# Last block of a Strassen-Winograd w_down product: another order of its seven products, a table of the side engines' work by step, and a fixed order for the finish of the output rows

## The chip, the core and the metric

One NeuronCore of a Trainium2 chip runs the whole kernel as one program. The metric is the device time of one execution in microseconds (us); smaller is better. Before the change three executions took 1968.8, 1969.25 and 1969.59 us; the median, 1969.25 us, is the time before.

## What is computed

The reference is one decoder layer in fp32 on 512 real tokens and 16 meta tokens of width 2048: RMSNorm, a combined input projection, sliding-window attention beside an mLSTM, an output projection with a residual, then

```python
u = rmsnorm(h, norm_mlp)
h = h + square(relu(u @ w_up)) @ w_down        # w_down: 8192 x 2048
h = rmsnorm(h, norm_final)
return h[:, BLOCK:]                             # 512 x 2048
```

The change touches the end of `@ w_down`, the last residual add and the final RMSNorm.

## The kernel before

Every fp32 product is made from three passes on TensorE: each operand is split into a rounded part `hi` (a cast on ScalarE, line 124) and a rest `lo` (a subtraction on VectorE, line 125), and `hi*hi + hi*lo + lo*hi` is accumulated in PSUM (lines 1086, 1089, 1090).

The `w_down` product runs over 16 blocks (`BLOCKS`, numbered 0 to 15 here): 8 chunks of the 8192 rows of `w_down` times two halves of the output columns. A block is a 2x2 Strassen-Winograd product: seven products (`ORDER`) instead of eight, each in two steps, so 14 steps m = 0 to 13. One step (`product`, L1067) is 12 matmuls with 512 columns. Its results gather in four PSUM tiles called X, W, Q and, in block 15, V (allocated under the name X), and from there in four quarters c00, c01, c10, c11 of the output, each 256 token rows by 512 columns.

What goes on beside the matmuls of step m is issued by `step` (L1098), and for block 15 by `last_step` (L1161):

- The operand of step m+2 is split (`weight_operand`, L1058): `hi(m+2)` on ScalarE, then `lo(m+2)` on VectorE. In this text hi(k) and lo(k) are the halves of the operand of step k of block 15. Three buffers hold such pairs, so hi(k) waits until TensorE is done with step k-3.
- Four of the seven weight operands are sums (`weight_sum`, L1052, the tiles t1 to t4, two halves each) of weight tiles y11, y12, y21, y22, made on VectorE (L1055). The weights come by DMAs that SP (SyncE) issues: `load_rows0` (L1027, tiles `raw`) and `load_rows1` (L1034, tiles `rh`); y12 of block 15 is loaded at step 7 of block 14.
- Finished quarters are copied or added out of PSUM (`add`, L1092) and accumulated into the DRAM tensors `hd` by a DMA with accumulation that POOL issues (`accumulate`, L1095); block 14 does so for c11 at step 11, c01 at step 12 and c10 at step 0 of block 15.
- In block 15 SP reads the sums back for the final norm: `load_h1(row, j)` (L1141) loads two tiles of 128 tokens by 512 columns into h1, `load_quarter` (L1146) the two column quarters that block 15 itself still adds to. h1(0, 1) can be read only when block 14's c01 has been accumulated, h1(1, 1) after its c11. ScalarE takes the sums of squares (`squares`, L1152, at line 708) and VectorE multiplies by the norm's weights (`weigh`, L1156).

TensorE, ScalarE and VectorE run in the order in which the code issues their instructions (`manual_schedule`, L1226), but only up to step 11 of block 15. SP and POOL are ordered by the scheduler, which lets a ready instruction pass one that is not ready: in `last_step(0)` the code issues `load_quarter(0, 1)` ahead of `load_quarter(1, 1)` and `load_h1(1, 1)`, and SP takes the latter two first.

After step 11 the rest is outside that order: `finish(b)` (L1198) for the four row blocks b, each a row scale on POOL (`v`, from the partial sums of squares, L1201 and L1202), two scaled tiles on ScalarE (L1204) and two on VectorE (L1208), each with its own output DMA of 256 KB (from ScalarE's queue L1205, from SP L1209). The last product (step 12 and 13) is done for the token half t = 0 into W and for t = 1 into V, and each half is added to c10 (L1093).

```python
LAST_ORDER = (0, 1, 5, 4, 2, 6, 3)
LAST_SUM_AT = {0: ("t2", 1), 3: ("t3", 0), 5: ("t3", 1), 6: ("t4", 0), 9: ("t4", 1)}
LAST_SRC = ("y11", "y21", "t2", "t1", "y22", "t3", "t4")
```

Of the kernel before, what the change touches and what calls it, by code (L numbers as in the profile page):

```python
# [10 lines left out]
F32 = mybir.dt.float32  # L11
# [6 lines left out]
P = 128  # L18
# [66 lines left out]
def hybrid_layer(ctx, tc, io, out):  # L85
# [959 lines left out]

    LASTB = len(BLOCKS) - 1
    LAST = STEPS * LASTB
    LAST_ORDER = (0, 1, 5, 4, 2, 6, 3)
    LAST_SUM_AT = {0: ("t2", 1), 3: ("t3", 0), 5: ("t3", 1), 6: ("t4", 0), 9: ("t4", 1)}
    LAST_SRC = ("y11", "y21", "t2", "t1", "y22", "t3", "t4")  # L1050

    def weight_sum(B, t, h):  # L1052
        dst = b3s.tile([P, 1024], F32, name="s", tag="s", bufs=5)
        in0, in1 = (wts[B, n, h] for n in SUM[t])
        dve.tensor_tensor(out=dst[:], in0=in0, in1=in1, op=ALU.subtract)  # L1055
        wts[B, t, h] = dst[:]
# [10 lines left out]
    def product(g, ts=(0, 1), hs=None):  # L1067
        B, m = divmod(g, STEPS)
        c, i = BLOCKS[B][0], m // 2
        if m == 0:  # L1070
            bks[B] = [dps.tile([P, 2, 512], F32, name=n, tag=n, bufs=2 if n == "X" else 1) for n in "XWQ"]
        if B == LASTB:
            if m == 8:
                bks[B].append(dps.tile([P, 2, 512], F32, name="X", tag="X", bufs=2))
            p, n, start = LAST_ORDER[i], (0, 1, 0, 2, 3, 0, 1)[i], i in (0, 1, 3, 4, 6)
        else:
            p, n, start = ORDER[i], (0, 1, 0, 2, 0, 2, 0)[i], i in (0, 1, 3)
        out = bks[B][n]
        for t in ts:
            for h in hs or (m % 2,):  # L1080
                wh, wl = ops[g - g % 2 + h]
                hi, lo = unit[c, p, h]
                for q in range(2):
                    a, a2 = (x[:, q * HTOK + t * P : q * HTOK + (t + 1) * P] for x in (hi, lo))
                    cols = slice(q * 512, (q + 1) * 512)
                    pe.matmul(  # L1086
                        out[:, t], a, wh[:, cols], start=start and h == q == 0, stop=False, skip_group_check=True
                    )
                    pe.matmul(out[:, t], a, wl[:, cols], start=False, stop=False, skip_group_check=True)  # L1089
                    pe.matmul(out[:, t], a2, wh[:, cols], start=False, stop=h == q == 1, skip_group_check=True)  # L1090
# [7 lines left out]
    def step(g):  # L1098
# [15 lines left out]
        if m in SUM_AT:  # L1114
            weight_sum(B, *SUM_AT[m])
        elif m == 13 and B < LASTB - 1:
            weight_sum(B + 1, "t1", 0)
        if g != 1:
            weight_operand(g + 2)
        if B == LASTB - 1 and m >= 12:  # L1120
            for t, h in ((("t1", 0),), (("t1", 1), ("t2", 0)))[m - 12]:
                weight_sum(B + 1, t, h)
        for mm, row, col in ((4, 0, 0), (11, 1, 1), (12, 0, 1)):
            if m == mm:
                add(cs[B, f"c{row}{col}"][:], (W if m == 4 else Q if m == 12 else cs[B, "c10"])[:])
# [5 lines left out]
            load_rows1(B + 1)  # L1131


    h1, nfs, last_sq = {}, [], {}

    def load_nf():
        for j in range(NJ):
# [3 lines left out]
    def load_h1(row, j):  # L1141
        h1[2 * row, j], h1[2 * row + 1, j] = unit_pair(len(keys_) + 2 * j + row, F32)
        for b in (2 * row, 2 * row + 1):
            sync.dma_start(out=h1[b, j], in_=hd[j][row][:, b % 2])

    def load_quarter(row, col):  # L1146
        d = quarter(LASTB, f"c{row}{col}")
        sync.dma_start(out=d[:], in_=hd[2 + col][row][:])
        for t in range(2):
            h1[2 * row + t, 2 + col] = d[:, t]  # L1150
# [5 lines left out]
    def weigh(row, j):  # L1156
        for b in (2 * row, 2 * row + 1):
            dve.tensor_tensor(out=h1[b, j], in0=h1[b, j], in1=nfs[j][:], op=ALU.mult)

    def last_step(m):  # L1160
        X, W, Q = bks[LASTB][:3]  # L1161
        if m == 0:
            act.copy(quarter(LASTB - 1, "c10")[:], bks[LASTB - 1][0][:])
            accumulate(LASTB - 1, 1, 0)
            load_h1(0, 0)
            load_quarter(0, 1)
            load_quarter(1, 1)
            load_h1(1, 1)
            load_h1(0, 1)
            load_h1(1, 0)  # L1170
            load_quarter(1, 0)
        elif m == 2:
            act.copy(quarter(LASTB, "c00")[:], X[:])
        if m in LAST_SUM_AT and m < 6:
            weight_sum(LASTB, *LAST_SUM_AT[m])
        if m < 12:
            weight_operand(LAST + m + 2)
        if m in LAST_SUM_AT and m >= 6:
            weight_sum(LASTB, *LAST_SUM_AT[m])
        for mm, row, j in ((1, 0, 0), (3, 1, 1), (4, 0, 1), (7, 1, 0), (10, 0, 2)):  # L1180
            if m == mm:
                squares(row, j)
        for mm, row, j in ((2, 0, 0), (5, 1, 1), (6, 0, 1), (8, 1, 0)):
            if m == mm:
                weigh(row, j)
        if m == 4:
            d = cs[LASTB, "c00"]
            add(d[:], W[:])
            pool.dma_start(out=hd[2][0][:], in_=d[:], accum_op=ALU.add)
            load_quarter(0, 0)  # L1190
        elif m in (7, 8, 10):
            add(cs[LASTB, "c01"][:], (X if m == 7 else Q if m == 8 else bks[LASTB][3])[:])
        elif m == 11:
            add(cs[LASTB, "c11"][:], Q[:])
            for b in range(2):
                last_square(b, 3)

    def finish(b):  # L1198
        tok = slice(b * P, (b + 1) * P)
        v = b3.tile([P, 1], F32, name=f"v{b}")  # L1200
        pool.tensor_tensor(out=v[:], in0=last_sq[b][:], in1=part[b][:], op=ALU.add)  # L1201
        pool.tensor_tensor(out=v[:], in0=v[:], in1=mhalf[:, :1], op=ALU.pow)  # L1202
        for j in (0, 1):
            act.activation(h1[b, j], h1[b, j], AF.Copy, scale=v[:])  # L1204
            act.dma_start(out=out[tok, j * 512 : (j + 1) * 512], in_=h1[b, j])  # L1205
        for j in (2, 3):
            h = h1[b, j]
            dve.scalar_tensor_tensor(out=h, in0=h, scalar=v[:], in1=nfs[j][:], op0=ALU.mult, op1=ALU.mult)  # L1208
            sync.dma_start(out=out[tok, j * 512 : (j + 1) * 512], in_=h)  # L1209

    part = {}

    def partial(b):
        part[b] = b3.tile([P, 1], F32, name=f"part{b}")
# [2 lines left out]
    def last_square(b, j):  # L1217
        last_sq[b] = b3.tile([P, 1], F32, name=f"sq{b}")
        act.activation(junk, h1[b, j], AF.Square, accum_out=last_sq[b][:])

    load_units(4 + FB)
    load_rows0(0, 0)
# [3 lines left out]
    with tc.manual_schedule(engines={mybir.EngineType.PE, mybir.EngineType.Activation, mybir.EngineType.DVE}):  # L1226
# [15 lines left out]
        for m in range(STEPS - 2):  # L1242
            product(LAST + m)
            last_step(m)
    X, W, _, V = bks[LASTB]
    for b in range(2):
        partial(b)
        finish(b)
    add(cs[LASTB, "c11"][:], X[:])
    add(cs[LASTB, "c10"][:], X[:])  # L1250
    squares(1, 3)
    for b in range(2, NB):
        partial(b)
    for t in range(2):
        bks[LASTB][1] = (W, V)[t]
        with tc.manual_schedule(engines=MAN):
            product(LAST + 12, (t,), (0, 1))
        add(cs[LASTB, "c10"][:, t], (W, V)[t][:, t])
        last_square(2 + t, 2)
        finish(2 + t)  # L1260


def layouts(inputs):
# [70 lines left out]
```

## Time and profile before

| what | value |
|---|---|
| median of three executions | 1969.25 us |
| the profiled execution's own time | 1968.98 us |
| its span, first to last instruction | 1967.2 us |
| TensorE busy | 1948.9 us, 99% of the span |
| VectorE busy / ScalarE busy / POOL busy | 1406.0 / 1010.8 / 238.8 us |
| mean granted TensorE clock | 0.998 of full speed |

All moments below are microseconds from the start of the span, so the last block of `w_down` lies near 1915 to 1953 and the end at 1967.2. A timeline row gives the start, the duration, the engine, the line, the operation with output and inputs, the shape, how many were merged, and in brackets the idle time before it and what ended that. Instructions of one engine overlap a little, so the distance between two starts is the price of one in a row of them.

### The profile page before, as it was taken

Reading aid. Unit: us, or ns where it says so; the run is one execution under the profiler, and the core shown is the slowest. Engines: PE = TensorE matmul, PEld = TensorE weight load, DVE = VectorE, ACT = ScalarE, POOL = GpSimd, SP = SyncE. Lnnn points to the kernel's source line nnn. Section 1 sums busy time; section 2 is a strip of 40 time slices with the busy share of each in tenths; the row PEclk is TensorE's granted clock in tenths of the full one; section 3 lists DMA queues with packets and bytes.
Section 4 is the critical chain, followed back from the end, with each engine's and each line's share of the span. In section 5 each row is a group of like instructions: output and inputs, shape, how many; then the busy total and the mean of one; then the engine's idle time right before and its main releaser. Section 6 shows DMA issues by size and latency. Waiting matters only on the chain.

```text
span 1967.2 us, 30626 instructions
## 1 busy us (share of the span) xinstructions
PE 1948.9 (99%) x12240; PEld 1745.6 (89%) x12240; DVE 1406.0 (71%) x1844; ACT 1010.8 (51%) x1491; POOL 238.8 (12%) x346
## 2 busy tenths in 40 slices
PE   9999999999999999999999999999999999999997
PEld 7878989988888899999999999998888888888885
DVE  6547773233644378787878787878888988888887
ACT  4433542245533255555555555556566566555655
POOL 0112220012111023222220000001100100010010
PEclk9999999999999999999999999999999999999999
DMA  8412112211243336555554444457878888888765
GB/s 316 135 65 88 65 65 76 91 70 65 86 171 130 127 137 210 191 187 187 188 184 166 157 166 153 169 167 253 212 217 224 227 222 215 226 208 203 223 171 187
DMA packets 112752, 324.61 MB, mean 165 GB/s; under 512 B 14016, under 2 KB 50496, under 8 KB 93648
## 3 DMA queue, kind: packets, MB, share of 16 engines
q1 hardware_dynamic: 65728, 245.55, 36.5%
q0 software_dynamic: 12320, 41.95, 10.9%
q10 hardware_dynamic: 34560, 35.14, 5.5%
q8 instruction: 96, 1.57, 0.3%
q14 instruction: 48, 0.39, 0.1%
HBM read 244.45 MB, written 78.15 MB: 164 GB/s over the span
## 4 chain that ended last, share of the span: by engine, by line
PE 69%; issue 24%; POOL 3%; DVE 2%; ACT 1%; DMA 1%; POOLq 0%; DVEq 0%; SPq 0%; ACTq 0%
PE g L171 10%; PE a L778 5%; PE g L778 5%; PE a L780 5%; PE a L779 5%; PE g L780 5%; PE g L779 5%; PE g L715 3%; PE g L717 3%; PE g L716 3%; PE g L186 2%; PE g L234 2%; POOL hd L1096 2%; PE g L184 2%; PE g L185 2%
## 5 line engine op out<-in xcount | busy, mean ns | idle before, releaser
L124 ACT CAST whi<-raw 128x1024 fp32r<-128x1024 f32 x224 | 235.3, 1050 | 405.3 <-PE g L717 85.5
L125 DVE TENSOR_TENSOR wlo<-raw,whi 128x1024 fp32r<-128x1024 f32 x224 | 274.6, 1226 | 201.5 <-ACT whi L124 196.5
L125 DVE TENSOR_TENSOR wlo<-s,whi 128x1024 fp32r<-128x1024 f32 x256 | 312.9, 1223 | 110.1 <-ACT whi L124 108.7
L124 ACT CAST whi<-s 128x1024 fp32r<-128x1024 f32 x256 | 269.0, 1051 | 209.5 <-PE g L779 62.1
L171 PE MATMUL g<-s,whi 128*128 128x264 f32 x1216 | 204.9, 287 | 0.2 <-DVE qa L270 0.2
L171 PEld LDWEIGHTS g<-s,whi 128*128 128x128 f32 x1216 | 170.9, 189 | 5.4 <-issue 4.9
L1089 PE MATMUL X<-wlo,s 128*128 128x512 f32 x356 | 138.6, 389 | 0.1
L1090 PE MATMUL X<-whi,s 128*128 128x512 f32 x356 | 138.5, 389 | 0.0
L1086 PE MATMUL X<-whi,s 128*128 128x512 f32 x356 | 138.5, 389 | 0.0
L171 PE MATMUL g<-s,wlo 128*128 128x264 f32 x608 | 128.0, 287 | 0.0
L778 PE MATMUL g<-y,whi 128*128 128x256 f32 x448 | 126.0, 281 | 1.0 <-ACT whi L124 1.0
L778 PE MATMUL a<-y,whi 128*128 128x256 f32 x448 | 125.6, 280 | 0.0
L779 PE MATMUL a<-s,whi 128*128 128x256 f32 x448 | 125.4, 280 | 0.0
L780 PE MATMUL a<-y,wlo 128*128 128x256 f32 x448 | 125.3, 280 | 0.0
L780 PE MATMUL g<-y,wlo 128*128 128x256 f32 x448 | 125.3, 280 | 0.0
L779 PE MATMUL g<-s,whi 128*128 128x256 f32 x448 | 125.3, 280 | 0.0
L779 PE MATMUL a<-y,whi 128*128 128x256 f32 x448 | 125.2, 280 | 0.0
L779 PE MATMUL g<-y,whi 128*128 128x256 f32 x448 | 125.2, 280 | 0.0
L780 PE MATMUL a<-s,wlo 128*128 128x256 f32 x448 | 125.2, 279 | 0.0
L778 PE MATMUL a<-s,whi 128*128 128x256 f32 x448 | 125.1, 279 | 0.0
L780 PE MATMUL g<-s,wlo 128*128 128x256 f32 x448 | 125.1, 279 | 0.0
L778 PE MATMUL g<-s,whi 128*128 128x256 f32 x448 | 124.8, 279 | 0.0
(371 smaller groups left out, 5099.2 us busy)
## 6 DMA issues: line engine op xcount, KB each, us to landing
raw<-in_w_dram SPq DMA_DIRECT2D x144, 1024.0 KB, 5.1
rh<-in_w_dram SPq DMA_DIRECT2D x64, 512.0 KB, 5.5
hd<-c POOLq DMA_DIRECT2D x61, 512.0 KB, 5.4
fu<-fd SPq DMA_DIRECT2D x108, 256.0 KB, 4.0
fd<-d ACTq DMA_DIRECT2D x32, 512.0 KB, 3.2
fd<-fs ACTq DMA_DIRECT2D x31, 512.0 KB, 3.5
xtok<-in_x_dram SPq DMA_DIRECT2D x4, 1024.0 KB, 11.6
hs<-in_x_dram SPq DMA_DIRECT2D x16, 256.0 KB, 5.8
```

The costliest lines, as they stand in the source:

```text
L124: act.copy(dst_hi, src)
L125: dve.tensor_tensor(out=dst_lo, in0=src, in1=dst_hi.bitcast(F32), op=ALU.subtract)
L171: pe.matmul(ps[s], w, x[:, PARTS[s]], start=first and kt == 0, stop=last and kt == KT - 1,)
L715: pe.matmul(ps[b][:], a, wh, start=kt == first, stop=False)
L716: pe.matmul(ps[b][:], a, wl, start=False, stop=False)
L717: pe.matmul(ps[b][:], c, wh, start=False, stop=kt == last)
L778: pe.matmul(out, wh, ah_, start=start and q == 0, stop=False, skip_group_check=True)
L779: pe.matmul(out, wh, al_, start=False, stop=False, skip_group_check=True)
L780: pe.matmul(out, wl, ah_, start=False, stop=q == KQ - 1, skip_group_check=True)
L1086: pe.matmul(out[:, t], a, wh[:, cols], start=start and h == q == 0, stop=False, skip_group_check=True)
L1089: pe.matmul(out[:, t], a, wl[:, cols], start=False, stop=False, skip_group_check=True)
L1090: pe.matmul(out[:, t], a2, wh[:, cols], start=False, stop=h == q == 1, skip_group_check=True)
```

## The change

Block 15 gets another order of products (p4 ahead of p5; p4 and p2 add up in Q, so that V holds only the last product's second half). VectorE's work by step is written in a table, with the squares of ScalarE beside it: those of (0, 0), (0, 1), (1, 1), (1, 0), (0, 2) stood at steps 1, 4, 3, 7, 10 and now follow the cast of steps 1, 2, 4, 6, 9. Block 14 makes the first three weight sums of block 15 at steps 8, 11 and 13 instead of 12, 13 and 13. The loads at the start of block 15 are issued in another order. The finish of all rows is moved into the fixed order of the three engines: that of rows 0 and 1 begins in step 11 (`first_rows`, ahead of hi(13) and lo(13)), the rest is written out in `last_rows`.

```diff
-    LAST_ORDER = (0, 1, 5, 4, 2, 6, 3)
-    LAST_SUM_AT = {0: ("t2", 1), 3: ("t3", 0), 5: ("t3", 1), 6: ("t4", 0), 9: ("t4", 1)}
-    LAST_SRC = ("y11", "y21", "t2", "t1", "y22", "t3", "t4")
+    LAST_ORDER = (0, 1, 4, 5, 2, 6, 3)
+    LAST_SRC = ("y11", "y21", "t1", "t2", "y22", "t3", "t4")
...
-            if m == 8:
+            if m == 12 and ts[0]:
                 bks[B].append(dps.tile([P, 2, 512], F32, name="X", tag="X", bufs=2))
-            p, n, start = LAST_ORDER[i], (0, 1, 0, 2, 3, 0, 1)[i], i in (0, 1, 3, 4, 6)
+            p, n, start = LAST_ORDER[i], (0, 1, 2, 0, 2, 0, (1, 3)[ts[0]])[i], i in (0, 1, 2, 6)
...
+        elif B == LASTB - 1 and m in (8, 11, 13):
+            weight_sum(B + 1, *{8: ("t1", 0), 11: ("t1", 1), 13: ("t2", 0)}[m])
         if g != 1:
             weight_operand(g + 2)
-        if B == LASTB - 1 and m >= 12:
-            for t, h in ((("t1", 0),), (("t1", 1), ("t2", 0)))[m - 12]:
-                weight_sum(B + 1, t, h)
...
+    LAST_DVE = (
+        (("sum", "t2", 1), ("lo",)),
+        (("lo",), ("sum", "t3", 0)),
+        (("lo",), ("weigh", 0, 0)),
+        (("lo",), ("weigh", 0, 1)),
+        (("lo",), ("add", "c00", 1)),
+        (("lo",), ("weigh", 1, 1)),
+        (("add", "c11", 2), ("lo",)),
+        (("lo",), ("sum", "t3", 1)),
+        (("add", "c01", 0), ("lo",), ("weigh", 1, 0)),
+        (("lo",), ("sum", "t4", 0)),
+        (("add", "c01", 2), ("lo",)),
+        (("sum", "t4", 1), ("first", 0), ("lo",)),
+    )
+    LAST_SQUARES = {1: (0, 0), 2: (0, 1), 4: (1, 1), 6: (1, 0), 9: (0, 2)}
...
-            load_h1(0, 0)
-            load_quarter(0, 1)
-            load_quarter(1, 1)
-            load_h1(1, 1)
-            load_h1(0, 1)
+            for j in range(2):
+                load_h1(0, j)
+            load_h1(1, 1)
+            load_quarter(1, 1)
+            load_quarter(0, 1)
             load_h1(1, 0)
             load_quarter(1, 0)
...
+            elif what == "lo":
+                weight_operand(LAST + m + 2)
+                if m in LAST_SQUARES:
+                    squares(*LAST_SQUARES[m])
...
+    def finish(b, js):
+        for j in js:
+            h, v = h1[b, j], scale[b]
+            if j < 2:
+                act.activation(h, h, AF.Copy, scale=v[:])
+            else:
+                dve.scalar_tensor_tensor(out=h, in0=h, scalar=v[:], in1=nfs[j][:], op0=ALU.mult, op1=ALU.mult)
+            (act if j < 2 else sync).dma_start(out=out[b * P : (b + 1) * P, j * 512 : (j + 1) * 512], in_=h)
+
+    def first_rows():
+        for b in range(2):
+            partial(b)
+            last_square(b, 3)
+            row_scale(b)
+        finish(0, (0,))
+
+    def last_rows():
+        c10, c11 = cs[LASTB, "c10"], cs[LASTB, "c11"]
+        X, W = bks[LASTB][:2]
+        finish(0, (1, 2))
+        add(c11[:], X[:])
+        finish(0, (3,))
+        finish(1, (0, 1))
+        add(c10[:], X[:])
+        squares(1, 3)
+        product(LAST + 12, (0,), (0, 1))
+        add(c10[:, 0], W[:, 0])
+        last_square(2, 2)
+        finish(1, (2,))
+        product(LAST + 12, (1,), (0, 1))
+        add(c10[:, 1], bks[LASTB][3][:, 1])
+        last_square(3, 2)
+        partial(2)
+        row_scale(2)
+        finish(1, (3,))
+        finish(2, (0, 2, 1, 3))
+        partial(3)
+        row_scale(3)
+        finish(3, (0, 2, 1, 3))
```

`partial(b)` is a small reduction on VectorE, `row_scale(b)` the two POOL instructions that give v; the old loop over `finish(b)` after step 11 is gone.

## Rows read from the trace of the kernel before

**Rows 1.** The page, part 1: the span, then busy time, share of the span and instructions of TensorE's matmuls (PE) and of the other engines.

```profile
span 1967.2 us, 30626 instructions
PE 1948.9 (99%) x12240; PEld 1745.6 (89%) x12240; DVE 1406.0 (71%) x1844; ACT 1010.8 (51%) x1491; POOL 238.8 (12%) x346
```

**Rows 2.** Busy time by stretch: the stretch, its length, then busy us and count of PE, its weight loads, DVE (VectorE), ACT (ScalarE) and POOL, the granted clock, the DMA engines' busy share and GB/s.

```profile
1888.00:1911.00 23.00, 23.00 (x103) 19.07 (x102) 16.52 (x14) 14.13 (x16) 0.86 (x1) 1.00 0.52 160
1930.00:1950.00 20.00, 20.00 (x90) 16.57 (x89) 20.00 (x24) 11.79 (x20) 1.27 (x2) 1.00 0.32 82
```

**Rows 3.** TensorE's timeline: the first matmul of block 15 and the last matmul of the kernel.

```profile
1915.19 0.39 PE L1086 MATMUL X<-whi,s 128*128 128x512 f32 x1
...
1953.05 0.39 PE L1090 MATMUL X<-whi,s 128*128 128x512 f32 x1
```

**Rows 4.** Who waited for whom from 1911 to the end: us in total, times, longest us. L708 are the squares, r are tiles of h1.

```profile
ACT s L708 <- DMA r<-hd: 2.1, 2, 1.2
```

**Rows 5.** The tail, from the timelines of VectorE, POOL, SP and ScalarE's queue: the second half of c10's last add; the row scale of row block 2; VectorE's scaled output tiles of rows 2 and 3; the first output DMA of those rows; the last two output DMAs of ScalarE's queue (their starts are the two figures behind the durations) and, from the same answer, the time from issue to landing.

```profile
1956.71 0.68 DVE L1093 TENSOR_TENSOR c<-c,X 128x512 f32<-128x512 f32 x1
...
1957.69 0.19 POOL L1201 TENSOR_TENSOR v<-sq,part 128x1 f32<-128x1 f32 x1 [6.23 <-ACT s L1219]
...
1958.54 2.74 DVE L1208 SCALAR_TENSOR_TENSOR c<-c,v,fu 128x512 f32<-128x512 f32 x4 [1.08 <-POOL v L1202]
...
1959.32 0.33 SPq L1209 DMA_DIRECT2D out_dram<-c  x1
...
L1205 ACTq DMA_DIRECT2D out_dram<-r x2: 982/1070/1159, 1960.7 to 1961.8; - x2
...
DMA to landing us min/median/max: 4.5/4.5/4.6
```

**Rows 6.** VectorE's timeline in block 14: the lo of step 9, the lo of step 10 (from a tile rh), and the add that completes c01.

```profile
1897.48 1.22 DVE L125 TENSOR_TENSOR wlo<-s,whi 128x1024 fp32r<-128x1024 f32 x1 [0.63 <-ACT whi L124]
...
1901.07 1.23 DVE L125 TENSOR_TENSOR wlo<-rh,whi 128x1024 fp32r<-128x1024 f32 x1 [2.36 <-ACT whi L124]
...
1913.36 1.21 DVE L1093 TENSOR_TENSOR c<-c,Q 128x1024 f32<-128x1024 f32 x1
```

**Rows 7.** SP's queue in block 14: what it waited for (us in total, times, longest), the first load of h1(0, 0), the load of y12 of block 15, and that load's time from issue to landing.

```profile
SPq L1144 <- DMA hd<-c: 18.1, 1, 18.1
...
1897.36 0.33 SPq L1144 DMA_DIRECT2D r<-hd  x1
1897.77 0.38 SPq L1030 DMA_DIRECT2D raw<-in_w_dram  x1
...
DMA to landing us min/median/max: 5.3/5.3/5.3
```

**Rows 8.** POOL's accumulating DMAs of block 14's c01 and c10, each with its time to landing, then SP's load of block 15's c01 quarter and of the two tiles of h1(0, 1), with the time to landing of these two.

```profile
1914.87 0.86 POOL L1096 DMA_DIRECT2D hd<-c  x1 [2.99 <-DVE c L1093]
...
DMA to landing us min/median/max: 5.1/5.1/5.1
...
1916.70 0.86 POOL L1096 DMA_DIRECT2D hd<-c  x1 [0.97 <-ACT c L1163]
...
DMA to landing us min/median/max: 10.5/10.5/10.5
...
1920.12 0.32 SPq L1148 DMA_DIRECT2D c<-hd  x1
...
1920.50 1.48 SPq L1144 DMA_DIRECT2D r<-hd  x2
...
DMA to landing us min/median/max: 8.5/8.5/8.6
```

**Rows 9.** DMA queues from 1927 to 1929: packets, MB, share of the 16 engines. q1 is SP's queue; POOL's queue, q0, has no row in that answer.

```profile
q1 hardware_dynamic: 365, 0.71, 95.6%
```

**Rows 10.** ScalarE's timeline in block 15: hi(5), and the first square of h1(0, 1).

```profile
1923.55 1.06 ACT L124 CAST whi<-s 128x1024 fp32r<-128x1024 f32 x1 [0.76 <-PE W L1090]
...
1929.17 0.63 ACT L708 ACTIVATE s<-r 128x512 f32<-128x512 f32 x1
```

**Rows 11.** VectorE's timeline in block 15: a weight sum, a pair of multiplications by the norm's weights, a lo, back to back.

```profile
1936.00 1.22 DVE L1055 TENSOR_TENSOR s<-rh,s 128x1024 f32<-128x1024 f32 x1
1937.13 1.28 DVE L1158 TENSOR_TENSOR r<-r,fu 128x512 f32<-128x512 f32 x2
1938.34 1.22 DVE L125 TENSOR_TENSOR wlo<-rh,whi 128x1024 fp32r<-128x1024 f32 x1
```

**Rows 12.** The finish of row block 0: VectorE's reductions, POOL's first instruction for its scale, ScalarE's two first scaled tiles, the first output DMA on ScalarE's queue, ScalarE's third scaled tile.

```profile
1948.61 0.22 DVE L1215 TENSOR_REDUCE part<-ssh 128x1 f32<-128x4 f32 x2
...
1949.59 0.41 POOL L1201 TENSOR_TENSOR v<-sq,part 128x1 f32<-128x1 f32 x1 [16.98 <-ACT s L1219]
...
1950.69 1.34 ACT L1204 ACTIVATE r<-r,v 128x512 f32<-128x512 f32 x2 [0.43 <-POOL v L1202]
1951.50 0.35 ACTq L1205 DMA_DIRECT2D out_dram<-r  x1
1951.93 0.71 ACT L1204 ACTIVATE r<-r,v 128x512 f32<-128x512 f32 x1
```

**Rows 13.** Busy time by stretch after the last matmul, columns as in the second group; the clock stands third from the right.

```profile
1956.00:1957.00 1.00, 0.00 (x0) 0.00 (x0) 0.96 (x4) 0.49 (x3) 0.00 (x0) 1.00 1.04 389
1957.00:1958.00 1.00, 0.00 (x0) 0.00 (x0) 0.46 (x2) 0.97 (x3) 0.23 (x2) 0.80 0.91 332
```

More of the change, by code (lines that the diff above doesn't have):

```diff
@@ L1131, in step @@
             load_rows1(B + 1)
-    h1, nfs, last_sq = {}, [], {}
+    h1, nfs = {}, []
     def load_nf():
@@ L1158, in weigh @@
             dve.tensor_tensor(out=h1[b, j], in0=h1[b, j], in1=nfs[j][:], op=ALU.mult)
+    LAST_DVE = (
[13 more added lines that the diff above has]
+    LAST_SQUARES = {1: (0, 0), 2: (0, 1), 4: (1, 1), 6: (1, 0), 9: (0, 2)}
     def last_step(m):
-        X, W, Q = bks[LASTB][:3]
         if m == 0:
@@ L1172, in last_step @@
         elif m == 2:
[L1173 to L1185, printed above, removed]
+            act.copy(quarter(LASTB, "c00")[:], bks[LASTB][0][:])
@@ L1186, in last_step @@
+        for what, *args in LAST_DVE[m]:
+            if what == "sum":
+                weight_sum(LASTB, *args)
+            elif what == "lo":
+                weight_operand(LAST + m + 2)
+                if m in LAST_SQUARES:
+                    squares(*LAST_SQUARES[m])
+            elif what == "weigh":
+                weigh(*args)
+            elif what == "first":
+                first_rows()
+            else:
+                add(cs[LASTB, args[0]][:], bks[LASTB][args[1]][:])
         if m == 4:
-            d = cs[LASTB, "c00"]
@@ L1188, in last_step @@
-            add(d[:], W[:])
-            pool.dma_start(out=hd[2][0][:], in_=d[:], accum_op=ALU.add)
+            pool.dma_start(out=hd[2][0][:], in_=cs[LASTB, "c00"][:], accum_op=ALU.add)
             load_quarter(0, 0)
[L1191 to L1209, printed above, removed]
@@ L1211, in hybrid_layer @@
-    part = {}
+    part, last_sq, scale = {}, {}, {}
     def partial(b):
@@ L1219, in last_square, with row_scale @@
         act.activation(junk, h1[b, j], AF.Square, accum_out=last_sq[b][:])
+    def row_scale(b):
+        scale[b] = v = b3.tile([P, 1], F32, name=f"v{b}")
+        pool.tensor_tensor(out=v[:], in0=last_sq[b][:], in1=part[b][:], op=ALU.add)
+        pool.tensor_tensor(out=v[:], in0=v[:], in1=mhalf[:, :1], op=ALU.pow)
+    def finish(b, js):
[3 more added lines that the diff above has]
+                act.activation(h, h, AF.Copy, scale=v[:])
+            else:
+                dve.scalar_tensor_tensor(out=h, in0=h, scalar=v[:], in1=nfs[j][:], op0=ALU.mult, op1=ALU.mult)
[29 more added lines that the diff above has]
+        finish(3, (0, 2, 1, 3))
     load_units(4 + FB)
@@ L1244, in hybrid_layer @@
             last_step(m)
[L1245 to L1260, printed above, removed]
+        last_rows()
 def layouts(inputs):
```

## The prediction

> **What bounds the kernel now.** TensorE's matmuls fill 99% of the span [rows 1], at the full granted clock and without a gap in the stretches shown of the last two blocks [rows 2]. So work on another engine costs or gives nothing there unless TensorE comes to wait for it. The matmuls start block 15 at 1915.19 and the last one starts at 1953.05 [rows 3]: 168 matmuls, 37.86 / 167 = 0.2267 us each, so a step of 12 takes 2.72 us, and TensorE ends at about 1953.3. From there to the end of the span at 1967.2 it does nothing. This tail of 13.9 us is all that can be shortened.
>
> In the tail the chain is: VectorE's add of c10's second half starts at 1956.71, 3.4 us after TensorE has ended; POOL's scale for row block 2 starts at 1957.69, VectorE multiplies with it from 1958.54, and the first output DMA of rows 2 and 3 leaves at 1959.32 [rows 5]. Eight DMAs of 256 KB follow; the last is issued at 1961.8 and lands 4.5 us later, at 1966.3. From the first of these DMAs to the end of the span are 7.9 us, which I take as fixed: the rows are the same 2 MB. **So the end is set by the moment at which the first DMA of rows 2 and 3 can leave**, and I follow that moment. VectorE is late because it is full: 20.00 us busy in the 20 us before 1950 [rows 2]. One reason is a stall of ScalarE, which waits 2.1 us in squares for tiles of h1 [rows 4] while the next cast stands behind them.
>
> **Part 1, weight sums earlier in block 14.** Two of three sums move to steps 8 and 11; the count is unchanged. Before, VectorE was free at 1897.48 + 1.13 = 1898.6, and the lo of step 10 ran at 1901.07 [rows 6]. The new sum at step 8 stands ahead of that lo and needs y12 of block 15. That load leaves SP at 1897.77, because SP had waited 18.1 us for an accumulation ahead of the first load of h1(0, 0), and lands 5.3 us later, at 1903.07 [rows 7]. Nothing in the change moves these two loads. So the sum starts at 1903.07, the lo of step 10 at 1904.20, done 1905.4. Step 10 of block 14 starts four steps before 1915.19, at 1904.31, and its second matmul, the first to read lo, at 1904.54. **TensorE waits 0.9 us.** If y12 came in time the price is 0. From 1903.07 VectorE is packed: the add that completes c01 is the eleventh instruction, at 1903.07 + 10 x 1.135 = 1914.4, 1.06 us later than 1913.36 [rows 6].
>
> **Part 2, loads and squares.** POOL's accumulation of c01 moves with that add from 1914.87 to 1915.9 and lands 5.1 us later, at 1921.0 [rows 8]. Only then can h1(0, 1) be read. In code it now stands first, but SP takes what is ready, and c11's tiles are ready a step earlier; so I put h1(1, 1) and the c11 quarter ahead of it, as they are now, and the c01 quarter, which left at 1920.12 ahead of it, behind. The two loads leave at about 1921.2 and 1921.9. With the 8.5 us of their row the second lands at 1930.4. From below: c10's accumulation runs from 1916.70 for 10.5 us, to 1927.2 [rows 8], and SP's queue has the engines to itself only after that [rows 9]; so not before 1927.3. Neither row is nearer; I take the middle, 1928.9.
>
> The squares of h1(0, 1) now follow hi(4) instead of hi(6), so hi(5), which ran at 1923.55 [rows 10], stands behind them. The last square starts at 1929.0 and takes 0.8 with its read; hi(5) runs 1929.8 to 1930.9, lo(5) to 1932.1. TensorE, shifted by 0.9, wants lo(5) at 1915.19 + 0.9 + 5 x 2.72 + 0.23 = 1929.9. **It waits 2.2 us** (0.6 at the lower bound, 3.7 at the upper). Behind hi(5) on ScalarE stands everything else, and VectorE, which waits for it, loses some 5 us from 1925.
>
> **Part 3, order of products and table.** One add of 1.13 us goes (c01 takes Q once for p4 + p2). From lo(5) on VectorE has eight lo, four adds, three sums and three pairs of norm multiplications until the partial sums of rows 0 and 1: 15 x 1.135 + 3 x 1.21 [rows 11] = 20.65 us, packed, so 1930.9 + 20.65 = 1951.55. The copies, loads and accumulations that only change place beside matmuls cost nothing: the other engines have idle time there, and their only path to the end is this list.
>
> **Part 4, rows 0 and 1 ahead of hi(13).** New is a wait: ScalarE must scale one tile of row 0 and issue its DMA before hi(13). POOL's scale took 1.1 us from its first instruction to ScalarE's start, and a scaled tile with its DMA issue keeps ScalarE from 1950.69 to 1951.93, 1.24 us [rows 12] (there the next tile ran meanwhile; in the laid down order the DMA waits for its tile and the queue behind it). So 1951.55 + 0.2 for the reductions [rows 12] + 1.1 + 1.24 = 1954.1; hi(13) ends at 1955.15, lo(13) at 1956.4. TensorE wants it in the middle of step 12 and 13's first half, at 1915.19 + 0.9 + 2.2 + 12 x 2.72 + 1.36 + 0.23 = 1952.5. **It waits 3.9 us**, and ends at 1953.3 + 0.9 + 2.2 + 3.9 = 1960.3.
>
> After such a gap 18 matmuls are left. After the last matmul of before the granted clock was still full (1.00, 2.4 GHz) from 1956 to 1957 and fell toward half (1.2 GHz) within the next microsecond [rows 13], though TensorE had stopped at 1953.3. The gap here is broken by one matmul, so the sum keeps the full clock. The Trainium skill (TensorE: Matmul & The Clock Gate, "HAM oscillation — how this bites in real kernels") says that a matmul engine left waiting between groups is throttled, so that the next group starts cold. No stretch shown here has matmuls after such a gap; by that rule the 18 would run at half speed, 18 x 0.2267 = 4.1 us longer, where by the row they keep their pace.
>
> **Part 5, the tail.** VectorE from lo(13)'s start at 1955.2: lo 1.13, three output tiles at 2.74 / 4 = 0.69, two adds of 1.13, c10's first half 0.68 = 6.1, so c10's second half at 1961.3, after TensorE's end. Then 0.68 for it and 0.2 for the reduction, which now stands behind this add though row block 2 needs only the first half; 0.85 on POOL and 0.78 to the first DMA, as in [rows 5]: 1963.8 against 1959.32.
>
> **Sum:** +4.5 us, so the profiled execution's 1968.98 would become 1973.5; the median was 0.27 above it, so 1973.8.
>
> **The rivals.**
>
> *The loads come in time* (not slower): SP takes h1(0, 1) first, or it lands by 1926, so ScalarE hardly waits. For it speaks the new order in the code; against it that SP now takes c11 before c01 though the code has them the other way. Then only the three-buffer rule holds: hi(9) starts with step 7 at 1934.4, lo(9) at 1935.5, and nine instructions at 1.135 and a pair at 1.21 lead to the partial sums at 1947.0, 4.55 us earlier than above. The wait before hi(13) stays. 4.5 - 4.55 gives nothing, so 1969.2; with y12 still late 1970.1. It decides if the second tile of h1(0, 1) lands before about 1927.
>
> *The tail pays in full*: also hi(13) comes in time. The first DMA of the last rows cannot leave before TensorE's end plus c10's half (0.2 to reach VectorE, 0.68, and 0.2 for the reduction) plus 0.85 plus 0.78 = 1953.3 + 2.7 = 1956.0, so at most 3.3 us are won: 1965.9. For it: VectorE has one add less. Against it: the row scale stands ahead of hi(13) in every case.
>
> *The clock falls* in the gap of part 4: c10's second half waits for TensorE until 1964.6 instead of 1961.3, +3.3, so 1977.1. Against it: that gap holds one matmul, and in [rows 13] the engine had also stood still before the microsecond that still has the full clock. The Trainium skill (TensorE: Matmul & The Clock Gate) would expect this rival.
>
> *One load only is late* (y12 in time, or h1(0, 1) at its lower bound): 1972.2 to 1972.9.
>
> **How the numbers follow.** 0.2%, 3.9 us, is about what a measurement of this kernel can tell from no change. The forecast has 0.48 (its own range, by the bounds of h1(0, 1), 1972.2 to 1975.3), the loads in time 0.30, one load late 0.08, the clock 0.07, the full tail 0.07. "Faster" means below 1965.3, just under the floor of 1965.9, and takes an error in my fixed terms: 0.04. "Slower" means above 1973.2: two thirds of the forecast's range and the clock, 0.39. The rest, 0.57, is within. The range, 1968.0 to 1976.0, takes in all but the full tail, the clock, and the edges of the two large cases.
>
> **What would show it.** In the profile after: a wait of VectorE for the `raw` load near 1903; TensorE with three waits, of about 0.9, 2.2 and 3.9 us, at step 10 of block 14, step 5 and the last product; squares at L708 waiting for `r` until 1929; ScalarE's cast behind POOL's v in step 11. If TensorE runs through to 1953.3, parts 1, 2 and 4 are wrong and the full tail holds. If the first DMA of rows 2 and 3 does not set the end by 7.9 us, part 5 is wrong.

## The result, and the profile after

The changed kernel takes 1976.68 us (median of six executions, 1975.63 to 1977.2) against 1969.11 for the kernel before in the same session: a ratio of 1.0038, 95% interval 1.0025 to 1.0051. It is slower by about 7.6 us. The forecast was 1973.8 us with a range up to 1976.0, and it put most of its chance on a difference within 0.2%; both are off, and one rival, the falling clock at 1977.1 us, is what happened. Two executions of the experiments, 5018.47 us with the squares exchanged and 2762.97 us with the old finish, stand far off; no ratio counts them, and without them the two medians would be 0.1 us lower.

The page, part 1 (answers to [rows 1]), and busy time by stretch (columns as in [rows 2]):

```profile
span 1975.4 us, 30627 instructions
PE 1953.2 (99%) x12240; PEld 1747.1 (88%) x12240; DVE 1405.1 (71%) x1843; ACT 1011.7 (51%) x1491; POOL 241.0 (12%) x346
```

```profile
1888.00:1911.00 23.00, 22.11 (x98) 18.00 (x97) 15.87 (x15) 13.22 (x15) 0.86 (x1) 1.00 0.47 126
1930.00:1950.00 20.00, 18.35 (x80) 14.64 (x79) 18.08 (x19) 12.79 (x24) 0.86 (x1) 1.00 0.39 107
1957.00:1962.00 5.00, 4.32 (x10) 3.46 (x11) 4.90 (x7) 2.89 (x6) 0.00 (x0) 0.50 0.71 263
```

The first two stretches were full before; now each has lost TensorE time. The third shows the granted clock at 0.50 while matmuls run. TensorE's waits from 1890 to the end (us in total, times, longest us), none of which the stretches before had:

```profile
PE W L1085 <- ACT whi L124: 2.7, 1, 2.7
PE Q L1088 <- DVE wlo L125: 1.6, 2, 0.9
PE Q L1085 <- ACT whi L124: 0.9, 1, 0.9
PE W L1088 <- DVE wlo L125: 0.8, 1, 0.8
```

**First wait.** VectorE's and SP's timelines in block 14. The load of y12 leaves at 1898.79, the sum that needs it starts 5.3 us later, and the lo of step 10 stands behind it ([rows 6] had it at 1901.07). TensorE waits 0.9 us.

```profile
1898.39 1.23 DVE L125 TENSOR_TENSOR wlo<-s,whi 128x1024 fp32r<-128x1024 f32 x1 [0.63 <-ACT whi L124]
1904.08 1.23 DVE L1054 TENSOR_TENSOR s<-raw 128x1024 f32<-128x1024 f32 x1 [4.46 <-DMA raw<-in_w_dram]
1905.23 1.22 DVE L125 TENSOR_TENSOR wlo<-rh,whi 128x1024 fp32r<-128x1024 f32 x1
...
1898.79 0.38 SPq L1030 DMA_DIRECT2D raw<-in_w_dram  x1
```

**Second wait.** SP's queue (h1(1, 1), then, behind the c11 quarter, h1(0, 1)), the landing of h1(0, 1), then ScalarE and VectorE. The squares wait 4.59 us, hi(5) stands behind them, lo(5) behind hi(5) ([rows 8, 10] are the rows of before).

```profile
1920.06 0.88 SPq L1142 DMA_DIRECT2D r<-hd  x2
...
1922.65 0.87 SPq L1142 DMA_DIRECT2D r<-hd  x2
...
DMA to landing us min/median/max: 6.7/6.9/7.0
...
1929.48 0.63 ACT L708 ACTIVATE s<-r 128x512 f32<-128x512 f32 x1 [4.59 <-DMA r<-hd]
...
1930.86 1.98 ACT L124 CAST whi<-s 128x1024 fp32r<-128x1024 f32 x2
...
1931.92 1.23 DVE L125 TENSOR_TENSOR wlo<-s,whi 128x1024 fp32r<-128x1024 f32 x1 [4.57 <-ACT whi L124]
```

**Third wait.** VectorE's partial sums, ScalarE's scaled tile with its DMA ahead of hi(13), then lo(13). Read downwards: sums, scale, tile, DMA, cast, lo.

```profile
1952.69 0.21 DVE L1209 TENSOR_REDUCE part<-ssh 128x1 f32<-128x4 f32 x2
...
1954.12 0.72 ACT L1224 ACTIVATE r<-r,v 128x512 f32<-128x512 f32 x1 [2.18 <-POOL v L1218]
1954.87 0.35 ACTq L1227 DMA_DIRECT2D out_dram<-r  x1
1955.32 1.04 ACT L124 CAST whi<-s 128x1024 fp32r<-128x1024 f32 x1 [0.48 <-ACT r L1224]
...
1956.40 1.23 DVE L125 TENSOR_TENSOR wlo<-s,whi 128x1024 fp32r<-128x1024 f32 x1 [3.50 <-ACT whi L124]
```

**The clock.** TensorE's last matmuls, and the granted clock by microsecond:

```profile
1953.30 0.39 PE L1089 MATMUL W<-whi,s 128*128 128x512 f32 x1
1956.42 0.50 PE L1085 MATMUL W<-whi,s 128*128 128x512 f32 x1 [2.73 <-ACT whi L124]
1957.68 0.80 PE L1088 MATMUL W<-wlo,s 128*128 128x512 f32 x1 [0.76 <-DVE wlo L125]
1958.27 0.63 PE L1089 MATMUL W<-whi,s 128*128 128x512 f32 x1
1958.70 0.63 PE L1085 MATMUL W<-whi,s 128*128 128x512 f32 x1
...
1963.79 0.39 PE L1085 MATMUL X<-whi,s 128*128 128x512 f32 x1
...
1964.25 0.40 PE L1089 MATMUL X<-whi,s 128*128 128x512 f32 x1
```

```profile
1956.00:1957.00 1.00, 0.50 (x1) 0.19 (x1) 0.60 (x1) 0.99 (x2) 0.00 (x0) 0.96 0.43 160
1957.00:1958.00 1.00, 0.32 (x1) 0.32 (x2) 1.00 (x2) 0.59 (x1) 0.00 (x0) 0.50 0.12 47
...
1964.00:1965.00 1.00, 0.65 (x3) 0.19 (x1) 0.31 (x1) 0.00 (x0) 0.00 (x0) 1.00 0.23 82
```

One matmul stands alone between two waits, the clock falls to its 1.2 GHz level, and the next ones run 0.43 us apart instead of 0.227; it is back at 2.4 GHz for the last three. From 1957.68 to 1964.25 the 16 steps take 6.57 us; at 0.227 they would take 3.63. So TensorE loses 2.9 us to the clock.

**The tail** (answers to [rows 5]): VectorE's last tile ahead of c10's second half, that half, POOL's scale and the first output DMA of rows 2 and 3.

```profile
1961.92 0.75 DVE L1226 SCALAR_TENSOR_TENSOR c<-c,v,fu 128x512 f32<-128x512 f32 x1
1964.69 0.69 DVE L1092 TENSOR_TENSOR c<-c,X 128x512 f32<-128x512 f32 x1 [2.02 <-PE X L1089]
...
1965.59 0.56 POOL L1217 TENSOR_TENSOR v<-sq,part 128x1 f32<-128x1 f32 x1 [10.97 <-DVE part L1209]
...
1967.57 0.37 ACTq L1227 DMA_DIRECT2D out_dram<-r  x1
```

From that first DMA to the end of the span are 1975.4 - 1967.57 = 7.8 us; before it was 7.9. So the end is again set by it, and it leaves 8.25 us later than the 1959.32 of before.

### The profile page after: what moved, and what is told of

It reads as the page before. It is cut to its first block, busy times and chain, and to the rows that moved or that the text cites. A ratio compares the mean times of both kernels' runs of the same rounds, so it can differ in the third digit from the quotient of the medians.

```text
span 1975.4 us, 30627 instructions
## 1 busy us (share of the span) xinstructions
PE 1953.2 (99%) x12240; PEld 1747.1 (88%) x12240; DVE 1405.1 (71%) x1843; ACT 1011.7 (51%) x1491; POOL 241.0 (12%) x346
## 4 chain that ended last, share of the span: by engine, by line
PE 69%; issue 24%; POOL 3%; DVE 2%; ACT 1%; DMA 1%; POOLq 0%; ACTq 0%; DVEq 0%
PE g L171 10%; PE a L778 5%; PE g L778 5%; PE a L780 5%; PE a L779 5%; PE g L780 5%; PE g L779 5%; PE g L717 3%; PE g L716 3%; PE g L715 3%; POOL hd L1095 2%; PE g L234 2%; PE g L186 2%; PE g L184 2%; PE g L185 2%
## 5 line engine op out<-in xcount | busy, mean ns | idle before, releaser
L1085 PE MATMUL X<-whi,s 128*128 128x512 f32 x348 | 136.1, 391 | 0.0
L1089 PE MATMUL X<-whi,s 128*128 128x512 f32 x348 | 136.0, 391 | 0.0
```

The lines of the kernel that those rows point to most:

```text
L1085: pe.matmul(out[:, t], a, wh[:, cols], start=start and h == q == 0, stop=False, skip_group_check=True)
```

## The experiments

All start from the changed kernel. Times are medians; each ratio is to the kernel before in the same session (1968.95 to 1969.55 us). Theory: three waits of TensorE, VectorE's list that starts late behind them, and the clock that falls in the third wait make up the loss.

**Fill the third gap.** Fifteen matmuls into a spare PSUM tile, issued where TensorE waits for hi(13); their result is not used.

```diff
+ if B == LASTB and m == 12 and t == 0 and h == 1:
+     fill = dps.tile([P, 2, 512], F32, name="Q", tag="Q", bufs=1)
+     for _ in range(15): pe.matmul(fill[:, 0], ...)
```

> The changed kernel with 15 matmuls more, put on TensorE between the two halves of the last product's first part, where TensorE waits 2.7 us for hi(13); they read operands that are there and write a PSUM tile that nobody reads. Theory A (three waits, and the clock that falls in the third): the clock stays at 1.00 behind the gap, the last 17 matmuls take 0.23 us instead of 0.43 us each, TensorE ends about 3 us earlier and c10's second half starts when VectorE is free, at about 1962.6 instead of 1964.7: about 2 us less than the changed kernel, 1974.6. Rival B (the lower clock hides behind VectorE's chain): as the changed kernel, 1976.7. Rival C (the extra work delays TensorE): 1977 or more.

Measured: 1974.36 us, ratio 1.0026 [1.0016, 1.0037]. TensorE's timeline and the stretch behind the gap:

```profile
1953.84 3.56 PE L1083 MATMUL Q<-whi,s 128*128 128x512 f32 x15
...
1958.04 0.50 PE L1092 MATMUL W<-wlo,s 128*128 128x512 f32 x1 [0.41 <-DVE wlo L125]
...
1958.00:1960.00 2.00, 1.96 (x8) 1.61 (x9) 2.00 (x3) 1.21 (x2) 0.00 (x0) 1.00 0.67 251
```

With more work the kernel is 2.3 us faster, and the clock is full. The intervals of the two ratios overlap (1.0025 to 1.0051 and 1.0016 to 1.0037), but the slowest execution with the gap filled, 1975.44 us, is faster than the fastest of the changed kernel, 1975.63, and the traces differ by 2.2 us behind a common mark (table below). So the clock's price is shown, at about 2.2 us.

**The scale behind hi(13).** Row 0's first scaled tile and its DMA move behind the cast.

```diff
             row_scale(b)
-        finish(0, (0,))
...
-        finish(0, (1, 2))
+        finish(0, (0, 1, 2))
```

> The changed kernel with the first scaled tile of row 0 and its output DMA moved behind hi(13) on ScalarE. Theory A: hi(13) starts when the sum t4 is there, near 1952.8 instead of 1955.3, TensorE waits about 1.2 us instead of 3.5, the clock stays at 1.00, and the first output DMA of rows 2 and 3 leaves about 5 us earlier: 1971.6. Rival B (that wait is VectorE's lateness and only changes its name): 1976 to 1977. Rival C (the clock falls all the same): about 1974.5.

Measured: 1971.55 us, ratio 1.0014 [1.0004, 1.0023]. The waits of the last product:

```profile
1952.68 0.50 PE L1085 MATMUL W<-whi,s 128*128 128x512 f32 x1 [0.25 <-ACT whi L124]
1953.94 0.51 PE L1088 MATMUL W<-wlo,s 128*128 128x512 f32 x1 [0.76 <-DVE wlo L125]
```

The gap is 0.25 + 0.76 us now, the clock stays full, and about 5 of the 7.6 us hang on the place of one tile. That is its price beside the other two waits, which are still in this kernel; by itself it costs less (third alone, below).

**The squares exchanged.** h1(1, 1) is squared at step 2 and h1(0, 1) at step 4, and their norm multiplications change places too. The median and the ratio are of the first run, the trace of a second one, of one execution.

```diff
-    LAST_SQUARES = {1: (0, 0), 2: (0, 1), 4: (1, 1), 6: (1, 0), 9: (0, 2)}
+    LAST_SQUARES = {1: (0, 0), 2: (1, 1), 4: (0, 1), 6: (1, 0), 9: (0, 2)}
```

> The changed kernel with the squares and norm multiplications of h1(1, 1) and h1(0, 1) exchanged, so that the tiles that land first are asked for first. Theory A: ScalarE waits until about 1927.4 instead of 1930.2, TensorE does not wait at step 5 (1.7 us before), VectorE is 2.5 us earlier from there on; the wait before hi(13) stays at about 3 us and may or may not drop the clock: 1974.2 if it falls, 1971 if it does not. Rival B (VectorE or the row scale sets the end whatever the squares do): 1976 to 1977.

> The kernel with the squares and norm multiplications of h1(1,1) and h1(0,1) exchanged, once more, for a profile that can be read. Theory A (ScalarE's cast stood behind a load that lands late; a step later the load is there): TensorE does not wait at step 5, keeps its 0.9 us in block 14 and a third wait of 2 to 3 us before the last product, in which the clock still falls; time 1971.5 to 1974. Theory B (any late square of h1 holds up the cast): the wait of 1.7 us only moves to another step.

Measured: 1972.82 us, ratio 1.0019 [1.001, 1.0029]; the second run took 1974.57 us, 0.6 above what was expected of it. The two may differ by the clock: the mean granted clock of the first run's nine executions lies between 0.998 (five of them, 1971.31 to 1973.3 us) and 0.996 (one, 1974.09), and the traced execution has 0.996. So the fall seems not to last equally long in every execution of this kernel, and the trace shows a long one; no other execution was traced. In the trace the squares still wait, but 2.06 us instead of 4.59; hi(5) comes in time, and only block 14's wait and the third one are left:

```profile
PE W L1085 <- ACT whi L124: 2.4, 1, 2.4
...
PE Q L1088 <- DVE wlo L125: 0.6, 1, 0.6
...
1926.92 0.63 ACT L708 ACTIVATE s<-r 128x512 f32<-128x512 f32 x1 [2.06 <-DMA r<-hd]
```

**The sums back.** Block 14 makes the three sums at steps 12 and 13 again.

```diff
-        elif B == LASTB - 1 and m in (8, 11, 13):
-            weight_sum(B + 1, *{8: ("t1", 0), 11: ("t1", 1), 13: ("t2", 0)}[m])
...
+        if B == LASTB - 1 and m >= 12:
+            for t, h in ((("t1", 0),), (("t1", 1), ("t2", 0)))[m - 12]:
+                weight_sum(B + 1, t, h)
```

> The changed kernel with the three weight sums of block 14 back at steps 12 and 13, behind the lo of the step. Theory A: no wait for y12, TensorE gains the 0.9 us at step 10 of block 14, c01 is accumulated about 1 us earlier and h1(0, 1) lands about 1 us earlier, the other two waits and the lower clock stay: 1975.7. Rival B (the sums that come back crowd VectorE at the start of block 15 as before and delay lo(4) to lo(6)): 1977 or more.

Measured: 1975.01 us, ratio 1.0029 [1.0019, 1.004]. The wait in block 14 is gone (TensorE is busy for all of the first stretch); the clock still falls, to 0.50 from 1956 to 1960:

```profile
1888.00:1911.00 23.00, 23.00 (x103) 19.06 (x102) 16.52 (x14) 14.16 (x16) 0.86 (x1) 1.00 0.52 160
1956.00:1960.00 4.00, 4.00 (x10) 3.13 (x11) 3.90 (x5) 2.56 (x6) 0.00 (x0) 0.50 0.85 318
```

The step of 1.7 us against the changed kernel is inside the intervals.

**All three undone.** The last three edits together (scale behind, squares exchanged, sums back); order of products, table and laid down finish stay.

> The changed kernel with all three waits undone together: block 14's sums back at steps 12 and 13, squares and norm multiplications of h1(1,1) and h1(0,1) exchanged, row 0's first scaled tile and its DMA behind hi(13). The new order of products, the table and the laid down finish stay. Theory A (the three waits of TensorE, and the clock that falls in the third, are the whole loss): TensorE runs through to 1953.3 at full clock; the partial sums of rows 0 and 1 come between 1947.0 (three-buffer rule) and 1949.5, and from them to the first output DMA of rows 2 and 3 it is 10.3 us in the run with the scale behind hi(13), so that DMA leaves at 1957.3 to 1959.8 (before: 1959.3) and the time is 1967 to 1969.5 us, no different from before. Theory B (the new order of products, the table or the laid down finish cost something by themselves): 1971 us or more.

Measured: 1967.76 us, ratio 0.9992 [0.9984, 1.0001]. TensorE has no wait from 1895 to the end; one stretch of it, which was 18.35 us busy in the changed kernel:

```profile
1930.00:1950.00 20.00, 20.00 (x90) 16.58 (x89) 18.05 (x21) 12.31 (x23) 1.76 (x5) 1.00 0.39 104
```

So nothing else in the change costs, on balance, anything that can be seen; theory B falls.

**Only the third wait, only the second.** The kernel with all three undone, with the scaled tile back ahead of hi(13); and with the squares as the change has them.

```diff
+        finish(0, (0,))        # third alone, behind row_scale(b)
...
+    LAST_SQUARES = {1: (0, 0), 2: (0, 1), 4: (1, 1), 6: (1, 0), 9: (0, 2)}   # second alone
```

> Of the three waits only the third is left: block 14's sums and the squares of h1 are undone, row 0's scaled tile and its DMA stay ahead of hi(13). The prediction's rival had this wait stay although the loads come in time. Theory A (the three waits add up; the third is due to the place of the scale): hi(13) starts at about 1951.2 on the clock of the kernel with all three undone (there 1948.78), TensorE wants it 1.2 us before it ends: TensorE waits about 1.2 us and 0.8 us for lo(13), the clock stays full, and as VectorE's packed list starts 2.4 us later the time is 2.4 us above the kernel with all three undone: 1970 us. Theory B (the clock falls in this gap too, so the third wait alone explains most of the loss): 1972 to 1974 us, with matmuls 0.43 us apart. Theory C (the third wait comes only from the lateness of the first two): 1967.8 us.

> Of the three waits only the second is left: block 14's sums are back at steps 12 and 13 and row 0's scaled tile stands behind hi(13), the squares of h1(0,1) stay ahead of hi(5). Theory A: TensorE waits 1.0 to 1.8 us at step 5, no wait or one under 1 us at the last product, clock full throughout; VectorE's packed list from lo(5) carries the delay to the end: 1.5 to 3.5 us above the kernel with all three undone, 1969.3 to 1971.3. Theory B (the second wait costs nothing without the first, because h1(0,1) then lands 1 us earlier): 1967.8.

Measured: third alone 1970.7 us, ratio 1.0006 [0.9997, 1.0015]; second alone 1972.06, ratio 1.0013 [1.0004, 1.0022], 0.8 us above the expected range. TensorE's waits and the clock, first with the third wait alone, then with the second alone:

```profile
1951.16 0.50 PE L1085 MATMUL W<-whi,s 128*128 128x512 f32 x1 [1.45 <-ACT whi L124]
1952.42 0.79 PE L1088 MATMUL W<-wlo,s 128*128 128x512 f32 x1 [0.76 <-DVE wlo L125]
...
1954.00:1956.00 2.00, 2.00 (x7) 1.58 (x6) 1.95 (x3) 1.55 (x4) 0.00 (x0) 0.54 1.00 366
```

```profile
1930.96 0.50 PE L1085 MATMUL Q<-whi,s 128*128 128x512 f32 x1 [0.94 <-ACT whi L124]
1932.22 0.50 PE L1088 MATMUL Q<-wlo,s 128*128 128x512 f32 x1 [0.76 <-DVE wlo L125]
...
1930.00:1934.00 4.00, 2.30 (x10) 1.66 (x10) 3.06 (x4) 3.97 (x7) 0.00 (x0) 1.00 0.50 186
```

Alone, the third wait is 1.45 + 0.76 us long, and the clock falls in it too, which theory A had not expected; only theory C is ruled out outright, and the 1970.7 lies between A and B. The clock is low for a shorter time here, eight matmuls instead of 14. Of the 3.2 us by which this trace ends later than that of all undone (table below), 2.5 come from the cast (VectorE stands idle 3.50 us ahead of lo(13), not 1.04) and 0.8 from the clock (VectorE then waits 0.77 us for TensorE ahead of c10's second half). The second wait, 0.94 + 0.76, leaves the clock full. But it costs more than TensorE's 1.7 us, and VectorE's list shows why. The moment at which POOL starts to accumulate block 14's c10 serves as a mark, since executions differ by up to 2 us before it. Mark and partial sums, for all three undone, then for the second wait alone:

```profile
1918.23 0.86 POOL L1095 DMA_DIRECT2D hd<-c  x1 [0.97 <-ACT c L1178]
...
1948.60 0.22 DVE L1210 TENSOR_REDUCE part<-ssh 128x1 f32<-128x4 f32 x2
```

```profile
1917.77 0.86 POOL L1095 DMA_DIRECT2D hd<-c  x1 [0.97 <-ACT c L1178]
...
1951.71 0.21 DVE L1210 TENSOR_REDUCE part<-ssh 128x1 f32<-128x4 f32 x2
```

30.4 us after the mark against 33.9: the second wait makes VectorE's list 3.6 us later, and this reaches the end whole. The same two moments in the other traces, us after each one's mark:

| kernel | waits left | partial sums | end of span | median us |
|---|---|---|---|---|
| before | none | 31.9 | 50.5 | 1968.95 to 1969.55 |
| changed | 1, 2, 3 | 33.9 | 56.6 | 1976.68 |
| third gap filled | 1, 2, 3, clock full | 33.7 | 54.4 | 1974.36 |
| scale behind hi(13) | 1, 2 | 34.0 | 52.2 | 1971.55 |
| squares exchanged (second run) | 1, 3 | 31.4 | 54.0 | 1974.57 (first run 1972.82) |
| sums back | 2, 3 | 34.3 | 56.7 | 1975.01 |
| second alone | 2 | 33.9 | 52.1 | 1972.06 |
| third alone | 3 | 30.4 | 51.8 | 1970.7 |
| all undone | none | 30.4 | 48.6 | 1967.76 |

The first wait lies ahead of the mark. Behind it, it makes the list 1.0 us later where the second wait is gone (31.4 against 30.4) and nothing where that is there, because the list then starts with the late hi(5) anyway. The ends show two things more. The changed kernel's lies 8.0 us behind that of all undone, and with the 0.9 us of the first wait, ahead of the mark, this is the 8.9 us between the two medians. And the waits do not simply add: the second and the third alone cost 3.5 and 3.2 us, both together (sums back) 8.1, mostly because the gap ahead of the last product is then longer and the clock low for longer (VectorE waits 1.80 us for TensorE there, 0.77 with the third alone).

**The finish.** On the kernel with all three undone: the old finish; then another order, with the partial sums of rows 2 and 3 and the scale of row block 2 early; then that with all output DMAs from SP; last, an order that also spreads rows 0 and 1.

```diff
+ # old finish, behind step 11 and outside the fixed order:
+ for b in range(2): partial(b); row_scale(b); finish(b, range(4))
+ # early scales, in last_rows
+ partial(2); partial(3)
+ product(LAST + 12, (0,), (0, 1)); add(c10[:, 0], W[:, 0])
+ last_square(2, 2); row_scale(2)
...
+ # rows spread: partial(0), partial(1) at step 10; ahead of lo(13):
+ finish(0, (2,))
+ # behind hi(13), all DMAs from sync:
+ finish(0, (0, 1)); finish(1, (0, 1))
```

> The kernel with the three waits undone, and besides the finish of all rows as it was before the change: the loop over row blocks after step 11, outside the fixed order, so that new are only the order of products and the table. Theory A (the laid down finish is worth nothing to either side; the end follows the moment at which VectorE comes to c10's halves): within 1.5 us of the kernel with the three waits undone, 1966.5 to 1969.5. Theory B (a fixed order, in which each output DMA of ScalarE's queue waits for its own tile, costs about 0.5 us per tile and makes rows 2 and 3 later): 2 us or more faster than that kernel.

> The kernel with the three waits undone, and its finish in another order: the partial sums of rows 2 and 3 ahead of c10's first half, the scale of row block 2 right behind its last square (not behind c10's second half), rows 0 and 1 filling the gaps of VectorE and ScalarE in between. If the tail is set by the chain c10's half, square, scale, first output DMA of rows 2 and 3, that DMA leaves at about 1957 and the last one lands at 1963 to 1965: 1965 to 1967 us. If the output DMAs themselves set it (4 MB at the 380 GB/s of the tail's rows are 11 us from the first one at about 1951): not below 1964. If neither the scale's place nor the order matters: the time of the kernel with the three waits undone.

> The same finish, with all sixteen output DMAs issued from SP, so that ScalarE's queue holds no DMA that waits for its own tile (a scaled tile with its DMA takes 1.15 us on ScalarE in the fixed order, 0.65 without). If ScalarE's queue is the last of the three to end in the tail: 1 to 2 us faster than the same finish with its own DMAs, 1964 to 1966 us. If the bytes set the end: the same time.

> The kernel with the three waits undone and another finish: the partial sums of rows 0 and 1 stand at step 10, one scaled tile of row 0 on VectorE fills its wait ahead of lo(13), ScalarE's four scaled tiles of rows 0 and 1 follow back to back behind hi(13), the scales of row blocks 2 and 3 stand right behind their last squares, all output DMAs go out from SP. In the two kernels with early scales the output's bytes set the end: the DMA engines stood still for parts of 1950 to 1955 and were then full until 1964. If so, feeding them from 1950 on without a hole (4.2 MB at 380 GB/s are 11 us) ends the span 2 to 3 us earlier than there, at 1964.0 to 1965.5 us time. If something else fixes the 11.4 to 12.2 us from TensorE's last matmul to the end (all four kernels with the waits undone showed them), the time stays at 1967.4 to 1967.8. If the tile ahead of lo(13) delays TensorE: 1 us or more slower.

Measured: old finish 1967.57 us, ratio 0.9992 [0.9983, 1.0001]; early scales 1967.44, 0.9991 [0.9982, 1.0]; from SP 1967.64, 0.9991 [0.9982, 1.0]; rows spread 1967.13, 0.9989 [0.998, 0.9998]. The ends lie 48.5, 48.6, 48.8 and 47.8 us after the mark. The laid down finish is worth nothing to either side, and neither the scale's place nor SP's queue moved the end by what was expected; the last kernel is the only one whose interval lies below 1, so it just beats the kernel before, by 0.1%, but not by the 2 to 3 us that a bound by bytes alone would have given. Its DMA engines by slices of 0.475 us from 1949, in busy tenths:

```profile
DMA  0019999999100099904999999999999600000000
```

They stand still from 1953.8 to 1955.6 and near 1957.3: no scaled tile is ready there. From 1957.5 to 1964 the engines are 97% busy at 362 GB/s, so there the bytes are the bound. What a feed without holes would give was not tried.

## Why the prediction was wrong

**The step that failed** is the last one of part 4: "The gap here is broken by one matmul, so the sum keeps the full clock." The clock fell in that gap, and a lone matmul between two waits did not keep it up. [rows 13] already showed the fall in the tail, in the microsecond after 1957; the forecast read from that row that the clock outlasts a stop, and took one matmul for work. The Trainium skill (TensorE: Matmul & The Clock Gate, "HAM oscillation — how this bites in real kernels") has the next group of matmuls start cold after a wait for data, in an example with longer, unbroken waits; here the trace agrees for the third wait, with matmuls 0.43 us apart, and not for the second, behind which the clock is full. The rival had the mechanism right and its size too large: TensorE lost 2.9 us, not 4.1, since the clock came back before the last three; VectorE's wait for it was 2.0 us, not 3.3, and filling the gap gave 2.3. That the rival's 1977.1 is so close to 1976.68 is luck: the other terms of the sum, which it shares with the forecast, were short, as follows.

**The first output DMA of rows 2 and 3** was put at 1963.8 and came at 1967.57. Of these 3.8 us, 0.9 lie ahead of the first instruction of block 14 that the change moves (1898.39 against 1897.48 for the lo of step 9); executions differ by as much there, and the 0.9 are none of the change's. lo(13) then started 0.3 later than put (1956.40 - 0.91 against 1955.2). The list from there to the end of the tile before c10's second half took 6.2 us instead of 6.1. The clock adds 2.1 (by the 0.66 us between two starts VectorE is free at 1962.58, and it starts at 1964.69). From that start to the DMA are 2.9 us instead of 2.5: POOL's first instruction took 0.56 us, in [rows 5] 0.19.

**Right, by the trace and by undoing each.** *Part 1*: y12's load holds up the sum, TensorE waits 0.9 us as put; that its removal saves as much could not be told from the times (1.0038 against 1.0029, and 1.0014 against 1.0013). *Part 2*: SP takes c11 first; hi(5) comes behind the squares of h1(0, 1) at 1930.86, which is 1929.95 on the clock of before, put at 1929.8; that figure rests on the middle between two bounds 3.1 us apart, so its closeness is in part luck; TensorE waits 1.7, put at 2.2. *Part 4*: scale, tile and DMA come ahead of the cast, and TensorE waits 3.5, put at 3.9. *Part 5*: the first DMA sets the end 7.8 us later, put at 7.9. This distance is not fixed, as part 5 took it to be: with early scales and with rows spread that DMA leaves 39.8 and 39.2 us after the mark, against 40.7 with all three undone, and the end comes 8.8 and 8.6 us behind it.

**The rivals.** "The loads come in time" fell with the landing of h1(0, 1). What it said of VectorE's list holds where the squares are exchanged (partial sums at 1948.60 - 1918.23 + 1916.70 = 1947.1 on the clock of before, with all three undone; put at 1947.0). Its price does not: with the first and the third wait left it has 1970.1 us, and that kernel, the squares exchanged, took 1972.82, the clock falling in its trace. "The tail pays in full" describes what the change could have given: with the waits undone it gives 1.5 us (with an interval that just takes in no difference), not 3.3. VectorE's list is still packed from lo(13) on and comes to c10's second half 0.8 us after TensorE's end, but that this is the reason is not shown: where the scale comes earlier, the end does not move with it. "One load only is late" did not occur.

**Chances.** The clock got 0.07 though the only row on it showed the fall within the tail; the forecast, standing 0.6 us above the bound of 0.2%, had little room for any term that was missed, and all of those missed lay on one side.

## What to carry to other kernels

An instruction put ahead of a cast in an engine's fixed order costs the wait of everything behind it: here a tile that waits for a scale, a square that waits for a load, and a sum that waits for a weight each held up the operand of the next product. A delay of a packed engine costs more than the wait that the bottleneck shows (3.6 us for 1.7), so follow the list to the end of the kernel. And where a wait is opened ahead of the last matmuls, price them at the lower clock, or fill it.

## What the runs showed of the hardware

- The granted clock fell to the 1.2 GHz level in gaps of 2.73 + 0.76 us and of 1.45 + 0.76 us, each broken by one matmul, and stayed full in gaps of 0.25 + 0.76 and of 0.94 + 0.76. In the changed kernel it came back at about 1963.6, after 14 matmuls 0.43 us apart; with the third wait alone after eight.
- Work without use kept the clock up: with fifteen matmuls in the gap the granted clock was 1.00 from 1958 to 1960, and the kernel was 2.3 us faster.
- On ScalarE, four scaled tiles back to back take 2.56 us (0.64 each, rows spread); with each one's DMA behind it in the same queue they start 1.14 us apart (all three undone). Moving all output DMAs to SP did not move the end (1967.64 us against 1967.44).
